# A hybrid layer pair on one core: the S5 stage in a written order without GpSimd, its Toeplitz matrices built through DRAM, and edits at both ends

## The chip, the cores and the metric

The kernel runs on one core of a Trainium2 chip. A core has five engines that run side by side: TensorE (PE, matrix products), VectorE (DVE), ScalarE (ACT), GpSimd (POOL) and SyncE (SP), which here only issues transfers; ACT issues a few as well. Engines wait for each other by semaphores, and each runs its own list of instructions strictly in order. The metric is the time of one execution on the device in microseconds (us).

## The reference

Depth is 2: one layer of native sparse attention (NSA), one S5 layer (a diagonal state-space mixer), and a last RMS norm, for 256 positions of width 1024, all in fp32. Cut to what the change touches:

```python
h = x + nsa(rmsnorm(x, l0_norm))                  # layer 0
xn = rmsnorm(h, l1_norm)                          # layer 1
u, z = split(xn @ w_in, 2)                        # 1024 columns each
# 64 groups of 16 columns, 64 complex states each: x_t = ab * x_{t-1} + bb @ u_t
y = real(C @ x_t) + d_skip * u
y = gelu(y)
ga, gb = split(y @ w_glu, 2)
h = h + (ga * sigmoid(gb) * silu(z)) @ w_out
out = rmsnorm(h, final_norm)
```

## The kernel before, in words

All products run on PE. A large product is done from fp32r pairs: the weights (`raw`, 512 KB pieces, four buffers) are split into a high part `wh` (an ACT copy, L207) and a low part `wl` (a subtraction, L209, on the engine whose turn it is in the list `lo_eng`), the activations likewise, and three products (L224 to L226, or L244 to L246 where the weights are the moving side) stand for one of full precision. Three buffers of `wh` and of `wl` go round. Products in plain fp32 (L267, 200 of them in the program, nearly all 128 by 256) use the raw weights as they are. Most of the program is ordered per engine by a scheduler at build time; inside a `manual_schedule` block the named engines keep the order of the code.

The attention layer fills the span to about 240 us. S5's parameters (the discretised states, the powers of the state matrix, `kt_` with the taps of each group) are worked out behind it by a background generator on POOL, DVE and small PE products; C's transposes (L544) are among them.

The S5 stage, from 242 us to the first product of `w_glu`:

- `u` in two halves of 512 columns (`proj_N`). Each half is transposed by DVE from PSUM and multiplied with the norm's row factors (L1368, L1369) into `ut`.
- A sequence is cut into chunks of 8 positions. Inside a chunk the contribution of `u` to `y` is one product with a Toeplitz matrix per group, `tm`. 32 transfers of SP (L1181) build `tm` out of `kt_`, SBUF to SBUF, in pieces of 64 to 512 bytes per row.
- From `ut` the inputs `v` of the scan come by products (L1305), an ACT copy `vs` (L1308), PE transposes (L1312) and copies on ACT and DVE (L1319, L1321). `scan_half` for each half of the groups (L1338 to L1358) rotates them, runs two first-order scans on DVE (L1344, L1345), rotates back (one multiplication on POOL, L1348) and writes the states `xf`.
- `z` in four tiles of 256 columns (`proj_T`, 48 products each), each scaled by DVE out of its PSUM bank (L1392), then tanh on ACT and a multiplication on DVE. In this stretch `lo_eng` is POOL alone.
- `y` in eight pieces (L1410 with the states, L1411 with `tm`), each transposed by DVE (L1413), gelu on ACT (L1416), split by DVE (L1417) and POOL (L1418).
- Then the products of `w_glu` (four pairs of tiles `gb`, `ga`), those of `w_out`, and the last norm with its stores.

The first norm (L332 on) squares both halves of x on ACT, and runs two chains of one-column DVE operations for the inverse root. The last norm multiplies with the norm's weights (`hg`, POOL) before the row factor is known, and stores the second half of the rows in eight pieces (L1469, L1471).

## Time and profile before

| | |
|---|---|
| median of 3 runs | 413.06 us (411.81, 413.06, 414.19) |
| the profiled execution | 414.05 us, its span 412.3 us |
| mean granted TensorE clock | 0.933 of full speed |
| busy, share of the span | PE 86%, DVE 55%, ACT 43%, POOL 65% |
| PE, from 258 to 334 us | waits of 19.7 us in all |
| PE, from 345 to 387 us | busy throughout |

Times on the trace count from the start of the span. What lies outside the span in the profiled execution is 414.05 - 412.3 = 1.75 us. A bracket at the end of a trace row gives the engine's idle time before it and what ended that. The clock is given as a share of 2.4 GHz: 0.50 is the lower of its two levels, 1.2 GHz.

### The profile page before, as it was taken

To read this page: it belongs to the slowest core of one execution; us is meant where nothing else is said; L and a number is where in the kernel's file an instruction comes from. 1 tells how busy PE (TensorE), PEld (TensorE's weight loads), DVE (VectorE), ACT (ScalarE), POOL (GpSimd) and SP (SyncE) were. 2 spreads that over 40 slices of the span, in tenths; PEclk is the share of its full clock that TensorE was granted. 3 is DMA by queue.
4 is the path that set the end of the run, shared out by engine and by line. 5 is a ranking of instruction groups with operands and counts; after the bars stand their busy time and mean duration, and the time that the engine had idled before them with its cause. 6 is when DMAs were issued, how large, how long until landed. Compare 5 with 4: busy or idle time off the path is not lost.

```text
span 412.3 us, 6834 instructions
## 1 busy us (share of the span) xinstructions
PE 354.2 (86%) x2505; PEld 293.0 (71%) x2505; DVE 227.9 (55%) x582; ACT 178.4 (43%) x397; POOL 269.3 (65%) x281
## 2 busy tenths in 40 slices
PE   3899599999999998968998879994858599999990
PEld 3688468865888787644766657783847599999890
DVE  4969904433355243524555498563999944264243
ACT  3212420145366467566784454342513335444432
POOL 7009459989987789999544489321872476665760
PEclk9699979999999999985999999998696899999996
DMA  8964315558633315411311335996741215655403
GB/s 256 158 172 114 110 53 153 152 190 244 181 103 99 106 57 178 126 52 51 103 36 58 113 103 99 172 87 180 251 156 54 71 34 158 199 163 200 152 2 102
DMA packets 59970, 52.03 MB, mean 126 GB/s; under 512 B 21928, under 2 KB 52704, under 8 KB 59872
## 3 DMA queue, kind: packets, MB, share of 16 engines
q1 hardware_dynamic: 49536, 50.41, 43.9%
q10 hardware_dynamic: 10400, 1.18, 2.2%
q8 instruction: 20, 0.33, 0.4%
q14 instruction: 14, 0.11, 0.1%
HBM read 48.17 MB, written 1.05 MB: 119 GB/s over the span
## 4 chain that ended last, share of the span: by engine, by line
PE 57%; DVE 16%; SPq 6%; POOL 6%; DMA 5%; issue 5%; ACT 3%; DVEq 0%; ACTq 0%; POOLq 0%
PE b L267 16%; SPq L1181 5%; PE b L280 4%; PE b L224 4%; PE b L225 4%; PE b L226 4%; PE ob L986 3%; PE tu L973 2%; PE b L246 2%; PE b L244 2%; PE b L245 2%; DVE pw L377 2%; POOL wl L209 2%; PE cm L745 2%; DVE bbT L1357 2%
## 5 line engine op out<-in xcount | busy, mean ns | idle before, releaser
L209 POOL TENSOR_TENSOR wl<-raw,wh 128x1024 fp32r<-128x1024 f32 x30 | 74.3, 2480 | 48.3 <-ACT wh L207 48.1
L267 PE MATMUL b<-xn,raw 128*128 128x256 f32 (+1 forms) x400 | 94.9, 390 | 4.7 <-DVE kl L795 3.4
L267 PEld LDWEIGHTS b<-xn,raw 128*128 128x128 f32 (+1 forms) x400 | 74.1, 190 | 18.6 <-issue 4.6
L207 ACT ACTIVATE wh<-raw 128x1024 fp32r<-128x1024 f32 x48 | 50.8, 1058 | 67.0 <-PE b L225 20.7
L209 DVE TENSOR_TENSOR wl<-raw,wh 128x1024 fp32r<-128x1024 f32 x18 | 26.3, 1462 | 26.3 <-ACT wh L207 26.3
L959 ACT ACTIVATE pt<-pt,nm 128x128 f32<-128x128 f32 (+1 forms) x64 | 28.3, 444 | 24.8 <-DVE nm L955 24.7
L225 PE MATMUL b<-yl,wh 128*128 128x256 f32 x128 | 36.1, 283 | 0.0
L224 PE MATMUL b<-yh,wh 128*128 128x256 f32 x128 | 36.1, 284 | 0.0
L226 PE MATMUL b<-yh,wl 128*128 128x256 f32 x128 | 36.0, 283 | 0.0
L975 DVE COPY pT<-tu 128x512 f32<-128x512 f32 x24 | 16.6, 691 | 25.4 <-PE tu L973 24.7
L968 ACT ACTIVATE pt<-pt,su 128x128 f32<-128x128 f32 (+1 forms) x64 | 24.6, 443 | 11.6 <-DVE su L966 11.5
L224 PE MATMUL b<-xp,wh 128*128 128x256 f32 x64 | 20.2, 317 | 5.7 <-ACT wh L207 5.7
L224 PEld LDWEIGHTS b<-yh,wh 128*128 128x128 f32 x128 | 24.5, 192 | 0.2 <-issue 0.2
L225 PEld LDWEIGHTS b<-yl,wh 128*128 128x128 f32 x128 | 24.6, 192 | 0.0
L226 PEld LDWEIGHTS b<-yh,wl 128*128 128x128 f32 x128 | 24.5, 192 | 0.0
L383 POOL TENSOR_TENSOR ep<-c1c,pw 128x1024 f32<-128x1024 f32 x8 | 16.0, 2022 | 10.3 <-ACT c1c L546 5.3
L955 DVE CUSTOM_DVE_ANT_0 pt<-su,b 128x128 f32<-128x128 f32 (+1 forms) x64 | 19.4, 351 | 4.7 <-PE su L943 4.7
L226 PE MATMUL b<-xp,wl 128*128 128x256 f32 x64 | 20.1, 316 | 1.6 <-POOL wl L209 1.6
L383 POOL TENSOR_TENSOR bbn<-bbn,bbt 128x512 f32<-128x512 f32 x16 | 20.4, 1274 | 0.6
L383 POOL TENSOR_TENSOR bbn<-b1c,h 128x512 f32<-128x512 f32 x16 | 17.8, 1111 | 4.6 <-PE bg L604 4.4
L986 PE MATMUL ob<-pT,vsw 128*64 128x128 f32 x192 | 17.4, 297 | 3.4 <-DVE pT L975 3.4
L225 PE MATMUL b<-xp,wh 128*128 128x256 f32 x64 | 19.8, 311 | 0.0
(319 smaller groups left out, 874.1 us busy)
## 6 DMA issues: line engine op xcount, KB each, us to landing
raw<-in_l_w_in_dram SPq DMA_DIRECT2D x44, 512.0 KB, 4.0
raw<-in_l_w_out_dram SPq DMA_DIRECT2D x16, 512.0 KB, 3.9
raw<-in_l_w_glu_dram SPq DMA_DIRECT2D x16, 512.0 KB, 3.6
raw<-in_l_cmp_k_w_dram SPq DMA_DIRECT2D x4, 512.0 KB, 3.9
raw<-in_l_cmp_v_w_dram SPq DMA_DIRECT2D x4, 512.0 KB, 3.9
xin<-in_x_dram SPq DMA_DIRECT2D x2, 512.0 KB
h<-in_x_dram SPq DMA_DIRECT2D x8, 128.0 KB, 3.3
tm<-kt__2197 SPq DMA_DIRECT2D x4, 128.0 KB
```

The lines of the kernel that those rows point to most:

```text
L207: A.activation(hi, raw, AF.Copy)
L209: lo_eng[-1].tensor_tensor(lo, raw, hi.bitcast(F32), op=ALU.subtract)
L224: T.matmul(dst, a, xh[:, k], start=(k == 0 and e == 0), stop=False)
L225: T.matmul(dst, a, xl[:, k], start=False, stop=False)
L226: T.matmul(dst, b, xh[:, k], start=False, stop=(k == KT - 1 and e == len(dsts) - 1))
L267: T.matmul(dst, w[:, i, e * m:(e + 1) * m], xn[:, k], start=(k == 0 and e == 0), stop=(k == KT - 1 and e == len(dsts) - 1))
L383: PL.tensor_tensor(o, a, b_, op=op)
L955: V.tensor_tensor_reduce(o.rearrange("p t k -> p (t k)"), sb[:, i * w + br * nk:i * w + (br + 1) * nk], self.b8[hf][:, S - nk:S], -0.125, ...
L959: A.activation(o, o, AF.Exp, scale=-1.0, bias=self.nm[:, j, hf, br:br + 1], accum_out=self.su[:, j, hf, br:br + 1])
L968: A.activation(o, o, AF.Copy, scale=r)
L986: T.matmul(self.ob[64 * hf:64 * hf + 64, j * P:(j + 1) * P], vsw[:, kt, br, 64 * g:64 * g + 64], p_, start=first, stop=last, tile_position ...
L1181: nc.sync.dma_start(tm[16 * s_:16 * s_ + 16, 16 * j:16 * j + 16].rearrange("p q l c -> p q (l c)")[:, :, 16 * l_:P], kt_[32 * j:32 * j + 1 ...
```

## The change

First norm: the square of the second half moves to DVE, the two chains take strict turns, and the first operations of S5's parameter chain, which the scheduler had mixed in, stand behind the norm. C's transposes get PSUM banks of their own. `kt_` is laid out anew; four transfers write it to DRAM (`kd`), and eight larger ones read `tm` from there.

The S5 stage is one block in a written order on PE, ACT, DVE and POOL. Products of `u`'s second half and of `v`, the scan and `z` are interleaved by hand. Tile 0 of `z` remains an fp32r product. For tiles 1 to 3 `x1_again` transposes the residual stream once more into `xf1`, and `z_products` multiplies it with the raw weights in plain fp32, 16 products for a tile, with no splits. The scan's multiplication on POOL goes to DVE, `y` is done in four pieces of 512 columns, gelu is evaluated twice by ACT (once into the high part), the low part is DVE's, and tanh with its multiplication (`z_gate`) moves into the loop of `w_glu`. The row of the last norm's weights, `gf`, is loaded into part of `tm` there. In the tail the second half of the rows is stored by four transfers, three of them on ACT's queue.

```diff
+        sums, ys = smp.tile([P, NQ], F32, name="ss0"), [[], []]
+        A.activation(sqs[:, 0], xin[:, 0], AF.Square, accum_out=sums[:, 0:1])
+        V.tensor_tensor_reduce(sqs[:, 1], xin[:, 1], xin[:, 1], 1.0, 0.0, ALU.mult, ALU.add, sums[:, 1:2])
+        for j in range(NQ):
+            for k in range(KT):
+                T.transpose(bts[k // 2][:, k % 2, j * P:(j + 1) * P], xin[:, j, k * P:(k + 1) * P], ident)
+        rq = [rsqrt_steps(sums[:, j:j + 1], ys[j]) for j in range(NQ)]
+        T.transpose(gb0[:, :KT], nrow, ident[:KT, :KT])
+        for r in rq * 12:
+            next(r, None)
+        for j in range(NQ):
+            row_bcast(*ys[j], rb[:, j * P:(j + 1) * P], cbias[:, j, 0:8].rearrange("p h n -> p (h n)"))
+        V.tensor_copy(g0c, gb0[:, :KT])
+        V.tensor_copy(rrow, rb[:, :S])
+        for k in range(KT):
+            V.scalar_tensor_tensor(xn[:, k], bts[k // 2][:, k % 2], g0c[:, k:k + 1], rrow,
+                                   op0=ALU.mult, op1=ALU.mult)
+        s5_loads()
+        chain = chain_gen()
+        for _ in range(3):
+            next(chain)
...
-            bt2 = bg_bank()
+            bt2 = bank(("tu", "ob")[q], 1)
...
-        kt_ = xp_.tile([P, 16, P], F32, name="kt_")
+        kt_ = xp_.tile([P, L, 16, 16], F32, name="kt_")
...
-            A.activation(kt_[:, ks_], kb, AF.Copy)
-            V.tensor_tensor(kt_[:, ks_, 0:16], kt_[:, ks_, 0:16], dk[:, ks_], op=ALU.add)
+            A.activation(kt_[:, :, ks_].rearrange("p d i c -> p i d c"), kb.rearrange("p i (d c) -> p i d c", d=L), AF.Copy)
+            V.tensor_tensor(kt_[:, 0, ks_], kt_[:, 0, ks_], dk[:, ks_], op=ALU.add)
...
-    tm = sl.tile([P, GS, L, 16], F32, name="tm")
+    tm = sl.tile([P, 4, L, 16, 16], F32, name="tm")
...
+    kd = kdp.tile([4, 16, L * 256], F32, name="kd")
+
     def toep_gen():
         kt_ = sh_ld["kt"]
+        for j in range(4):
+            nc.sync.dma_start(kd[j], kt_[32 * j:32 * j + 16].rearrange("p l i c -> p (l i c)"))
+        yield
         for s_, l_ in enumerate(SLOT_L):
-            for j in range(4):
-                nc.sync.dma_start(
-                    tm[16 * s_:16 * s_ + 16, 16 * j:16 * j + 16].rearrange("p q l c -> p q (l c)")[:, :, 16 * l_:P],
-                    kt_[32 * j:32 * j + 16, :, 0:P - 16 * l_])
-                if j % 2:
-                    yield
+            nc.sync.dma_start(tm[16 * s_:16 * s_ + 16, :, l_:L].rearrange("p j l i c -> p j (l i c)"),
+                              kd[:, :, 0:(L - l_) * 256].rearrange("j p x -> p j x"))
+            if s_ % 2:
+                yield
...
+    def u_evac(cc):
+        uh = ut[:, 32 * cc:32 * cc + 32]
+        V.transpose(uh, ubs[cc].rearrange("p j (g c) -> p g j c", c=16))
+        V.tensor_tensor(uh, uh, rcolT.unsqueeze(1).to_broadcast([P, 32, NCH]), op=ALU.mult)
...
-        for q in range(2):
-            for u in range(2):
-                for ri in range(2):
+                T.transpose(vb[:, q, t * P:(t + 1) * P], vss[hg][q][:, t], ident)
+        for ri in range(2):
+            for q in range(2):
+                for u in range(2):
                     o = vh[hg][64 * u:64 * u + 64, ri, 256 * q:256 * q + 256].rearrange("p (t x) -> p t x", t=2)
                     i_ = vb[64 * ri:64 * ri + 64, q].rearrange("p (t u x) -> p u t x", u=2, x=P)[:, u]
-                    if q == 0:
+                    if q == 0 or hg:
...
-        PL.tensor_tensor(b_, c_, b_, op=ALU.mult)
         V.tensor_tensor(w2_, s_, a, op=ALU.mult)
+        V.tensor_tensor(b_, c_, b_, op=ALU.mult)
...
+    def x1_again(cc):
+        b = bank2(psu["pool"]).rearrange("p e (k s) -> p (e k) s", k=2)
+        for j in range(NQ):
+            for i in range(4):
+                T.transpose(b[:, i, j * P:(j + 1) * P], h1s[j][:, 512 * cc + i * P:512 * cc + (i + 1) * P], ident)
+        for i in range(4):
+            A.activation(xf1[:, 4 * cc + i], b[:, i], AF.Copy, scale=colsT[:, 4 * cc + i:4 * cc + i + 1])
+
+    def z_products(c2):
+        zb = bank().rearrange("p (e s) -> p e s", e=2)
+        for k0 in range(0, KT, 4):
+            w = load_w(w_in1, k0, 4, D + 256 * c2, 2 * P)
+            for i in range(4):
+                k = k0 + i
+                for e in range(2):
+                    T.matmul(zb[:, e], w[:, i, e * P:(e + 1) * P], xf1[:, k], start=(k == 0 and e == 0),
+                             stop=(k == KT - 1 and e == 1))
+        return zb
+
+    def z_scaled(c2, zb):
+        V.tensor_tensor(z2[:, 2 * c2:2 * c2 + 2], zb, rrow.unsqueeze(1).to_broadcast([P, 2, S]), op=ALU.mult)
+
+    def z_gate(c2):
+
+        th = wk.tile([P, 2, S], F32, tag="sg", name="th", bufs=2)
+        zt = z2[:, 2 * c2:2 * c2 + 2]
+        A.activation(th, zt, AF.Tanh, scale=0.5)
+        V.scalar_tensor_tensor(zt, th, 1.0, zt, op0=ALU.add, op1=ALU.mult)
...
+        V.transpose(ytf, yb)
+        A.activation(yhl[0][:, qs_], yt, AF.Gelu_apprx_tanh)
+        A.activation(yt, yt, AF.Gelu_apprx_tanh)
+        V.tensor_tensor(yhl[1][:, qs_], yt, yhl[0][:, qs_].bitcast(F32), op=ALU.subtract)
...
+    with tc.manual_schedule(engines={E_.PE, E_.Activation, E_.DVE, E_.Pool}):
+        u_evac(0)
+        for _ in range(2):
+            next(gen_u1)
+        v_products(0)
+        next(gen_u1)
+        v_transposed(0)
+        for _ in gen_u1:
+            pass
+        zb = bank().rearrange("p (e s) -> p e s", e=2)
+        gen_z = proj_T_steps([zb[:, 0], zb[:, 1]], w_in1, D, P, xh1, xl1)
+        for _ in range(4):
+            next(gen_z)
+        scans = [scan_steps(0), scan_steps(1)]
+        u_evac(1)
+        next(scans[0])
+        v_products(1)
+
+        sh_ld["xm"].__exit__(None, None, None)
+        sh_ld["bp"].__exit__(None, None, None)
+        rs.__exit__(None, None, None)
+        wk = ctx.enter_context(tc.tile_pool(name="wk", bufs=1, reuse_waits="tile"))
+        xf1 = wk.tile([P, KT, S], F32, name="xf1")
+        z2 = wk.tile([P, KT, S], F32, name="z2b")
+        x1_again(0)
+        for _ in gen_z:
+            pass
+        for _ in toep:
+            pass
+        hooks.clear()
+        x1_again(1)
+        v_transposed(1)
+        next(scans[0])
+        next(scans[0])
+        z_scaled(0, zb)
+        zb = z_products(1)
+        next(scans[1])
+        z_scaled(1, zb)
+        yb = [y_products(q2) for q2 in range(2)]
+        for q2 in range(2):
+            y_gelu(q2, yb[q2])
+        zb = z_products(2)
+        next(scans[1])
+        next(scans[1])
+        z_scaled(2, zb)
+        zb = z_products(3)
+        yb = [y_products(q2) for q2 in range(2, 4)]
+        for q2 in range(2, 4):
+            y_gelu(q2, yb[q2 - 2])
+        z_scaled(3, zb)
+    yh, yl = yhl
...
-    with tc.manual_schedule(engines={E_.PE, E_.Activation}):
-        v_half(0)
-        v_half(1)
-    for hg in range(2):
-        scan_half(hg)
-    lo_eng[:] = [PL]
...
-        zb = bank().rearrange("p (e s) -> p e s", e=2)
-        proj_T([zb[:, 0], zb[:, 1]], w_in1, D + 256 * c2, P, xh1, xl1)
-        if c2 == 0:
-            hooks.clear()
-            for _ in toep:
-                pass
-            dump("tm", tm)
-            sh_ld["xm"].__exit__(None, None, None)
-            sh_ld["bp"].__exit__(None, None, None)
-            rs.__exit__(None, None, None)
-            wk = ctx.enter_context(tc.tile_pool(name="wk", bufs=1, reuse_waits="tile"))
-            z2 = wk.tile([P, KT, S], F32, name="z2b")
-        zs = wk.tile([P, 2, S], F32, tag="zs", name="zs", bufs=1)
-        V.tensor_tensor(zs, zb, rrow.unsqueeze(1).to_broadcast([P, 2, S]), op=ALU.mult)
-        zt = z2[:, 2 * c2:2 * c2 + 2]
-        A.activation(zt, zs, AF.Tanh, scale=0.5)
-        V.scalar_tensor_tensor(zt, zt, 1.0, zs, op0=ALU.add, op1=ALU.mult)
...
-        V.transpose(yt, yb[:, :S])
...
-        V.tensor_copy(yh[:, qd], yt)
-        PL.tensor_tensor(yl[:, qd], yt, yh[:, qd].bitcast(F32), op=ALU.subtract)
...
+    lo_eng[:] = [V, V] + [PL, PL, V] * 10
...
+    gf = tmf[:, 4 * D:5 * D]
     for c2 in range(4):
+        z_gate(c2)
+        if c2 == 1:
+            nc.sync.dma_start(gf, fnorm.unsqueeze(0).to_broadcast([P, D]))
...
-        if i == 4:
+        if i >= 3:
...
-        V.scalar_tensor_tensor(ho[1][:, 768:D], h1s[1][:, 768:D], y, gf[:, 768:D], op0=ALU.mult, op1=ALU.mult)
-        V.tensor_scalar(ho[1][:, 512:768], hg[1][:, 512:768], y, None, op0=ALU.mult)
+        V.scalar_tensor_tensor(ho[1][:, 512:D], h1s[1][:, 512:D], y, gf[:, 512:D], op0=ALU.mult, op1=ALU.mult)
         for l_ in range(4):
-            nc.sync.dma_start(o3[1, l_, :, 0:512], ho[1][32 * l_:32 * l_ + 32, 0:512])
-        for l_ in range(4):
-            (nc.scalar, nc.sync)[l_ % 2].dma_start(o3[1, l_, :, 512:D], ho[1][32 * l_:32 * l_ + 32, 512:D])
+            (nc.sync if l_ == 1 else nc.scalar).dma_start(o3[1, l_], ho[1][32 * l_:32 * l_ + 32])
```

Three places show what the order becomes. The first is DVE where the first half of `u` leaves PSUM (bank `b_2189` before, `b_2191` after; the second half is `b_2453`); `wl` are the low parts, the first two of each list those for the second half's first weights. Before:

```order
L639 TENSOR_TENSOR kt__2197<-kt__2197,dk 128x4x16
L209 TENSOR_TENSOR wl<-raw,wh 128x1024 x2
L1368 STREAM_TRANSPOSE ut<-b_2189 128x1024
L209 TENSOR_TENSOR wl<-raw,wh 128x1024
L1369 TENSOR_TENSOR ut<-ut,rcolT 128x1024
L209 TENSOR_TENSOR wl<-raw,wh 128x1024
L1368 STREAM_TRANSPOSE ut<-b_2453 128x1024
```

And after:

```order
L645 TENSOR_TENSOR kt__2199<-kt__2199,dk 128x64
L1304 STREAM_TRANSPOSE ut<-b_2191 128x1024
L1305 TENSOR_TENSOR ut<-ut,rcolT 128x1024
L214 TENSOR_TENSOR wl<-raw,wh 128x1024 x3
L1334 COPY bbT_88<-b_2558 64x256 x4
L214 TENSOR_TENSOR wl<-raw,wh 128x1024 x2
L1304 STREAM_TRANSPOSE ut<-b_2453 128x1024
```

Two low parts that stood ahead of the evacuation of `u` now stand behind it, and the fourth stands behind the four copies of `v`.

The second place is ACT from the weights of `u`'s second half to those of `z`. `vs` and `bbT_88` are the two evacuations of `v`, `xf` the second transposition of the residual. Before:

```order
L1289 ACTIVATE rrow<-b_2416 128x256
L207 ACTIVATE wh<-raw 128x1024 x3
L1308 ACTIVATE vs<-b_2539 128x512
L1308 ACTIVATE vs<-b_2558 128x512
L1319 ACTIVATE bbT_88<-b_2538 64x256 x4
L1308 ACTIVATE vs<-b_2594 128x512
L1308 ACTIVATE vs<-b_2613 128x512
L207 ACTIVATE wh<-raw 128x1024
```

And after:

```order
L1296 ACTIVATE rrow<-b_2418 128x256
L1318 ACTIVATE vs<-b_2500 128x512
L1318 ACTIVATE vs<-b_2519 128x512
L212 ACTIVATE wh<-raw 128x1024
L1332 ACTIVATE bbT_88<-b_2558 64x256 x4
L212 ACTIVATE wh<-raw 128x1024 x2
L1318 ACTIVATE vs<-b_2637 128x512
L1318 ACTIVATE vs<-b_2656 128x512
L1384 ACTIVATE xf_2681<-b_2683,colsT 128x256 x4
L212 ACTIVATE wh<-raw 128x1024
```

High parts that were made in one run ahead of `v` now each stand behind an evacuation.

The third place is PE behind the first half of `z`'s tile 0 (`b_2595`), up to the first plain product of tile 1 and `y`. Before, PE went from `v` to `z` (`b_2683`) like this:

```order
L246 MATMUL b_2453<-wh,xp_2274 128x512
L1305 MATMUL b_2539<-bbT_208,ut 32x128 x12
L1305 MATMUL b_2558<-bbT_88,ut 32x128 x16
L1312 MATMUL b_2538<-ident,vs 128x128 x8
L1305 MATMUL b_2594<-bbT_88,ut 32x128 x8
L1305 MATMUL b_2594<-bbT_1040,ut 32x128 x8
L1305 MATMUL b_2613<-bbT_1040,ut 32x128 x16
L224 MATMUL b_2683<-xp_2162,wh 128x256
```

After, two pieces of its list, the first at the middle of tile 0, the second at its end:

```order
L231 MATMUL b_2595<-xp_2164,wl 128x256
L1315 MATMUL b_2637<-bbT_88,ut 32x128 x8
L1315 MATMUL b_2637<-bbT_1039,ut 32x128 x8
L1315 MATMUL b_2656<-bbT_1039,ut 32x128 x16
L1382 MATMUL b_2683<-ident,h_93 128x128 x8
L229 MATMUL b_2595<-xp_2276,wh 128x256
```

```order
L231 MATMUL b_2595<-xp_2276,wl 128x256
L1382 MATMUL b_2726<-ident,h_93 128x128 x8
L1325 MATMUL b_2739<-ident,vs 128x128 x8
L1393 MATMUL b_2767<-xf_2681,raw 128x256 x16
L1419 MATMUL b_2796<-ep,bbT_88 32x8x16
```

The products of `v`'s second half moved between the halves of tile 0, 16 transposes of the residual (L1382) are new, and a tile of `z` is one run of 16 products.

## Rows read from the trace of the kernel before

**Rows 1.** PE's waits, 258 to 334 us: total us, times, longest

```profile
PE b L1410 <- DVE zs L1392: 11.8, 2, 7.2
PE b L224 <- ACT wh L207: 5.7, 1, 5.7
PE b L226 <- POOL wl L209: 1.6, 1, 1.6
```

**Rows 2.** Windows: stretch, length, busy of each engine, clock, DMA share, GB/s

```profile
285.00:295.00 10.00, 5.79 (x25) 5.50 (x26) 5.94 (x6) 5.69 (x9) 7.32 (x4) 0.51 0.93 312
310.00:316.00 6.00, 4.69 (x33) 4.28 (x34) 6.00 (x7) 1.58 (x2) 2.95 (x1) 0.51 0.02 4
326.00:330.00 4.00, 3.49 (x75) 3.38 (x79) 3.44 (x7) 2.64 (x4) 0.68 (x1) 0.57 0.42 123
345.00:387.00 42.00, 42.00 (x325) 40.81 (x324) 14.73 (x13) 19.43 (x22) 29.20 (x14) 1.00 0.60 188
```

**Rows 3.** PE's own timeline: start, duration, instruction, idle time before

```profile
86.34 3.62 PE L267 MATMUL b<-xn,raw 128*128 128x256 f32 x16
...
271.26 1.44 PE L1312 MATMUL b<-ident,vs 128*128 128x128 f32 x8
...
281.48 0.28 PE L225 MATMUL b<-xp,wh 128*128 128x256 f32 x1
281.60 0.28 PE L226 MATMUL b<-xp,wl 128*128 128x256 f32 x1
...
333.86 0.38 PE L224 MATMUL b<-yh,wh 128*128 128x256 f32 x1
```

**Rows 4.** The page's costliest groups, the plain fp32 products

```profile
L267 PE MATMUL b<-xn,raw 128*128 128x256 f32 (+1 forms) x400 | 94.9, 390 | 4.7 <-DVE kl L795 3.4
```

**Rows 5.** SP's queue, 250 to 292 us, and the DMA packets, 248 to 300

```profile
252.86 6.59 SPq L1181 DMA_DIRECT2D tm<-kt__2197  x8
...
262.45 19.85 SPq L1181 DMA_DIRECT2D tm<-kt__2197  x22
282.40 2.19 SPq L193 DMA_DIRECT2D raw<-in_l_w_in_dram  x4
...
DMA packets 12915, 8.18 MB, mean 157 GB/s; under 512 B 7856, under 2 KB 12464, under 8 KB 12848
```

**Rows 6.** DVE's timeline, 258 to 317 us

```profile
258.23 1.24 DVE L1368 STREAM_TRANSPOSE ut<-b 128x1024 f32<-128x1024 f32 x1
259.40 1.18 DVE L209 TENSOR_TENSOR wl<-raw,wh 128x1024 fp32r<-128x1024 f32 x1
260.50 1.21 DVE L1369 TENSOR_TENSOR ut<-ut,rcolT 128x1024 f32<-128x1024 f32 x1
...
274.32 1.74 DVE L1321 COPY bbT<-b 64x256 f32<-64x256 f32 x4 [1.35 <-ACT bbT L1319]
279.12 0.69 DVE L1343 TENSOR_TENSOR bbT<-bbT 128x512 f32<-128x512 f32 x1
...
313.57 2.87 DVE L1343 TENSOR_TENSOR bbT<-bbT 128x512 f32<-128x512 f32 x1
```

**Rows 7.** POOL's timeline at the same time

```profile
312.94 2.95 POOL L209 TENSOR_TENSOR wl<-raw,wh 128x1024 fp32r<-128x1024 f32 x1 [6.76 <-ACT wh L207]
```

**Rows 8.** ACT's timeline, 268 to 275 us

```profile
268.39 1.06 ACT L207 ACTIVATE wh<-raw 128x1024 fp32r<-128x1024 f32 x1 [2.50 <-DMA raw<-in_l_w_in_dram]
...
271.40 0.60 ACT L1308 ACTIVATE vs<-b 128x512 f32<-128x512 f32 x1 [0.28 <-PE b L1305]
272.74 1.55 ACT L1319 ACTIVATE bbT<-b 64x256 f32<-64x256 f32 x4 [0.75 <-PE b L1312]
```

**Rows 9.** SP's queue, 400 us to the end

```profile
405.29 1.76 SPq L1463 DMA_DIRECT2D out_dram<-tm  x4
...
409.15 0.84 SPq L1471 DMA_DIRECT2D out_dram<-tm  x2
```

**Rows 10.** What PE waited for, whole span

```profile
PE bg L544 <- DVE pT L494: 1.2, 1, 1.2
```

More of the change, by code (lines that the diff above doesn't have):

```diff
@@ L179, in s5_loads @@
             nc.scalar.dma_start(cnat[:, :, i], cc.rearrange("(t g) c p -> (g c) t p", t=8))
+    att = tc.tile_pool(name="att", bufs=1, reuse_waits="tile")
+    atp = att.__enter__()
+    cbias = atp.tile([P, NQ, 16, NB], F32, name="cbias")
     hooks = []
```

134 lines of the change are left out of this document (54 added, 80 removed).

## The prediction

> **What bounds the kernel now.** I read the windows first. From 345 to 387 us, in the products of `w_glu` and `w_out`, PE is busy for 42.00 of 42 us [rows 2]. So whatever the stage ahead gains or loses arrives at the end nearly undiminished: the end is the first product of `w_glu`, at 333.86 us [rows 3], plus a fixed run of work. Hence the second view, what PE waited for on its way there: 11.8 us in two waits for DVE to scale `z` out of its bank, 5.7 us for a high part of weights, 1.6 us for a low part by POOL [rows 1], 19.1 us together. Third, the windows behind these waits: the clock stands at 0.51 from 285 to 295 us and from 310 to 316 us and at 0.57 from 326 to 330 us [rows 2], so that products cost twice their time there. Half of PE's busy time in them is such excess: 2.9 + 2.3 + 1.7 = 6.9 us.
>
> The views of the other engines say why PE waited. SP issued 22 of the Toeplitz transfers from 262.45 on, for 19.85 us, and the weights that `z` waited for only at 282.40; 7856 of 12915 packets were under 512 B, at a mean of 157 GB/s [rows 5]. And DVE's one addition of 128 by 512 took 0.69 us at 279.12, but 2.87 us at 313.57 [rows 6], beside POOL's split of 2.95 us [rows 7]. The scan was slow where POOL split weights, and `z`'s scaling stood behind the scan.
>
> **The change, part by part: the stage.** Counted on PE from 258 us to the first product of `w_glu`, as differences; the products of `u`, `v`, tile 0 and `y` remain.
>
> Plain `z` products. Before, a tile is 48 products that follow each other by 0.12 us (281.48 to 281.60 [rows 3]), 5.8 us. The page lists 400 rows for L267 [rows 4] where the program has 200 products: each fp32 product is two rows. So the 16 rows of 3.62 us [rows 3] are 8 products, at 0.43 to 0.45 us each, and a tile of 16 is 6.9 to 7.2 us. That is 1.1 to 1.4 us more on PE, three times: +3.4 us at the lower end. The edit saves splits, not PE.
>
> Second transposition of the residual: 16 transposes; eight took 1.44 us, the last one's tail included [rows 3]. +2.2 us.
>
> Waits. POOL's splits and the late weights go: DVE's scan runs at 0.69 us an operation, and 32 issues of SP become 12. The bytes are not fewer: eight reads of 2.4 MB at 157 GB/s [rows 5] take 15 us, at the 312 GB/s of the window at 285 [rows 2] 8 us, behind four writes. They start about 253 us, like the transfers of before [rows 5], and end by 268 to 275 us, while `tm` is wanted by `y`, about 300 us; the weights of tile 0 queue behind them and are wanted about 280 us (258 plus the products and waits below). I cost the trip through DRAM at nothing, hidden by the products of `u` and `v`; without that cover it is up to 10 us.
>
> In their place come waits that the written order makes, since a low part stands behind an evacuation on DVE, and a high part on ACT, each ahead of the next piece of PE's work. First, the second half of `u`: its first low part stands behind transpose 1.24, multiplication 1.21, then takes 1.18 [rows 6]; less 0.3 us of PE work beside, 3.2 us. Before, PE did not wait there, the low parts being ready. Second, its third weights: a copy 0.60, the high part 1.06 [rows 8], the low part 1.18, and a handing over, 3.0 us. Third, its fourth weights: four copies of 1.55 on ACT [rows 8] and four of 1.74 on DVE [rows 6] take turns, then 1.06 and 1.18, of which 0.8 overlaps; with handings over 5.0 us. Fourth, the second half of tile 0: two `vs` copies and four copies of `xf` by ACT, 2.9 us of which PE's transposes cover 1, then 1.06 and 1.18, 3.8 us. Together 15.0 us for 19.1, -4.1 us; by the rows I allow 11 to 19 us. Behind that, I see PE busy without a wait through tiles 1 to 3 and `y`: from the fourth wait to the second half's states DVE has some 34 operations of 0.7 to 1.2 us, 26 us (my estimate from [rows 6]), and PE three tiles, 20.7 us, and beside them half of tile 0 (2.9), 16 transposes (2.2) and half of `y`.
>
> Clock. The 6.9 us of excess go if no wait lets the clock fall: -6.9 us. But four waits of 3 to 5 us are the kind that made it fall before: the wait of 5.7 us and those of 7.2 and 4.6 us [rows 1] each have a half-rate window behind them [rows 2]. No row has one of 3 to 4 us here. Each fall costs 1.7 to 2.9 us, by those windows. I take 3.0 us, for one or two falls of four (0 to 9).
>
> The Trainium skill (TensorE: Matmul & The Clock Gate, HAM oscillation) says that waits between short bursts of products can throttle the engine again at every turn. By that rule all four waits cost, 9 us in place of 3, and the sum below would be 6 us higher; the trace agrees where it shows waits of 4.6 us and more.
>
> The `gf` load. ACT's scaling of that row (1.06 us by ACT's split of the same size [rows 8]) stands ahead of high parts of the second tile of `w_glu`, and its load can be issued only when PE has read `tm` for the last time. ACT, the high part behind it and POOL's low part follow one another, 1.06 + 1.06 + 2.95 [rows 7], and PE has 72 products of 0.12, 8.6 us, until it wants them. With a landing of 3.5 us that fits; with one of 8 it costs 4.5. I take 0.9, a fifth of that (0 to 5).
>
> Sum of the stage: 3.4 + 2.2 - 4.1 - 6.9 + 3.0 + 0.9 = -1.5 us.
>
> **The tail.** Before, SP issued the first rows' four stores until 407.05 and the last of the others until 409.99 [rows 9], and the span ended 2.3 us later. Now ACT's queue issues three and SP one, when the wide multiplication is done about 406.2. At 0.44 us an issue (1.76 for four [rows 9]) both end about 407.6. -2.3 us, with the same landing; larger stores landing later could take 0.5 back.
>
> **The start.** C's transposes waited 1.2 us for a shared bank [rows 10]; with banks of their own PE goes on. The norm's chain is free of the parameter operations, which come later instead and can hold back POOL's work. I take -1.2 us, the wait alone, between -3 and +1.5, as the scheduler mixes the rest anew.
>
> Together -1.5 - 2.3 - 1.2 = -5.0 us: 409.05 us against the profiled 414.05. That execution lies 1 us above the median, so 408.0 us.
>
> **The rivals.** *The clock holds.* Waits of 3 to 5 us pass without a fall and `gf` lands early: 3.9 us less, and if three of the waits are a microsecond shorter, 6.9 less: 401 to 404 us. For it speaks that PE runs dense between the waits; against it, all rows of waits above 4.5 us.
>
> *Slower.* The clock falls at each of the four waits, since each comes within 7 us of the last and PE never recovers: 12 us of half-rate excess in place of 3, and so 9 us on the forecast: 417 us, with nothing else gone wrong. It decides when the excess passes 8 us, from where on the sum is above the old time. Against it: behind the fourth wait PE has over 26 us of dense work, and in the rows the clock was back within 10 us.
>
> *The gain is eaten in the stage.* DRAM's round trip makes tile 0's weights late by 5 us, or POOL's leftover low part holds the scan: 412 to 413 us, no change. Against it stands the room of 5 to 12 us for the load.
>
> **How the numbers follow.** A measurement of this kernel tells no change from about 0.5%, 2.07 us. The forecast, a gain of 2 to 8 us (405 to 411), has 0.47; the clock holding, or a stage better than I count, 0.24; the gain eaten 0.16; slower 0.13. Of the forecast 0.02 reaches into the middle band, so faster has 0.69, same 0.18, slower 0.13. The range leaves out the best of the second case and most of the slower one: 400.5 to 414.0 us; the forecast's own is 404 to 411.
>
> **What would show it.** Right: SP's queue done with `tm` by 264 us; no DVE addition of 128 by 512 above 1 us beside POOL; rows of a `z` tile of 16 products summing to 6.9 us at full clock; PE waiting for low parts four times between 258 and 295 us, 3 to 5 us each; the last store issued about 2.3 us sooner after the last product. The clock in the windows behind each wait decides between the cases. Wrong: PE waiting for `xf` or a bank in tiles 2 and 3 (DVE is then the bound), `tm`'s landing after 290 us, or waits by PE of over 5 us in `w_glu`'s first tiles behind `gf`.

## The result, and the profile after

The changed kernel is slower: 426.2 us (median of 4, 424.55 to 429.0) against 412.83 (4 runs, 411.81 to 414.19) beside it on the same chip, a ratio of 1.0322 (95% interval 1.0294 to 1.0351). Forecast were 408.0 us, within 400.5 to 414.0. The profiled execution took 425.98 us, its span 424.2. Of the runs below, two of e1's four executions, one of e6's four (the one that was profiled, so its trace is not read) and one of e13's six lay more than 1.5% above the fastest of their kernel, and their times and ratios are given without these.

To see where the 11.9 us of span went, I read the same seven events in both traces, in us from the start of the span. The last column is by how much the stretch that ends there grew.

| event | before | after | stretch |
|---|---|---|---|
| first product of the first projection | 13.11 | 11.83 | -1.3 |
| PE goes on after its wait for `kl`, the keys' low parts | 50.58 | 58.42 | +9.1 |
| PE's wait for `nm` ends, in late attention | 187.97 | 195.73 | -0.1 |
| last broadcast behind `u`'s first half | 257.56 | 268.20 | +2.9 |
| first product of `w_glu` | 333.86 | 340.87 | -3.6 |
| last residual addition starts | 402.73 | 413.76 | +4.0 |
| end of the span | 412.3 | 424.2 | +0.9 |

So the S5 stage, to which most of the prediction went, did become shorter. The loss lies in the start (+7.8 net of the faster norm), in late attention, in `w_glu` and at the end.

**The start.** DVE's timeline ahead of `kl`, before:

```profile
47.13 0.43 DVE L377 TENSOR_TENSOR c<-pw 128x256 f32<-128x256 f32 x1
47.59 0.42 DVE L377 TENSOR_TENSOR pw<-pw,c 128x256 f32<-128x256 f32 x1
48.05 0.63 DVE L532 COPY h<-pw 128x128 f32<-128x128 f32 x4
```

The same operations after:

```profile
49.07 0.41 DVE L339 TENSOR_TENSOR pw<-pw,c 128x256 f32<-128x256 f32 x1
...
49.85 2.13 DVE L339 TENSOR_TENSOR c<-pw 128x256 f32<-128x256 f32 x1
52.02 2.13 DVE L339 TENSOR_TENSOR pw<-pw,c 128x256 f32<-128x256 f32 x1
54.18 2.34 DVE L538 COPY h<-pw 128x128 f32<-128x128 f32 x4
```

GpSimd's timeline there, before and after, a row each (three such products follow one another, in 5.97 and 6.37 us):

```profile
48.62 2.02 POOL L383 TENSOR_TENSOR ep<-c1c,pw 128x1024 f32<-128x1024 f32 x1 [5.33 <-ACT c1c L546]
```
```profile
49.66 2.04 POOL L345 TENSOR_TENSOR ep<-c1c,pw 128x1024 f32<-128x1024 f32 x1 [3.65 <-DVE pw L339]
```

And what PE waited for, before and after:

```profile
50.58 4.90 PE L267 MATMUL b<-xn,raw 128*48 128x256 f32 x11 [3.43 <-DVE kl L795]
```
```profile
58.42 1.91 PE L272 MATMUL b<-xn,raw 128*48 128x256 f32 x4 [12.42 <-DVE kl L798]
```

Before, GpSimd starts 0.02 us after DVE's `kl`, which begins at 48.60, when the last table operations are done. After, it starts at 49.66, ahead of them, and they last as long as its own products, 2.13 us in place of 0.42. `kl` stands behind them on DVE, and PE waits 12.42 us.

So it is not that GpSimd starts earlier: it starts 1.0 us later than before. Before, what released it last was ACT's `c1c`, which ended at 48.49 us; in the changed kernel `c1c` ends at 48.60, but the table comes 2.7 us later (its last `c<-pw` begins at 47.13 and at 49.85), and now GpSimd is ahead of the table's end. The two rows of 2.13 and the one of 2.34 us are 5.1 us longer than before; with the 2.7 that is the whole 7.8.

The trace of before shows the same meeting further up in the same chain. Two equal operations of the table, the second beside a product of GpSimd:

```profile
38.78 0.21 DVE L377 TENSOR_TENSOR pw<-pw,c 128x64 f32<-128x64 f32 x1
...
41.11 2.26 DVE L377 TENSOR_TENSOR pw<-pw,c 128x64 f32<-128x64 f32 x1
```
```profile
40.88 2.42 POOL L383 TENSOR_TENSOR h<-h,ep 128x1024 f32<-128x1024 f32 x1
```

**The stage.** PE's waits from 268.2 to 340.87 us (engine, line, what for: us in all, times, longest), where before had those of [rows 1]:

```profile
PE b L249 <- ACT wh L212: 5.3, 2, 3.6
PE b L250 <- DVE wl L214: 4.8, 3, 3.3
PE b L229 <- ACT wh L212: 2.6, 1, 2.6
PE b L231 <- DVE wl L214: 0.8, 1, 0.8
```

Four waits, 13.5 us together; the single ones of 0.8 come right behind one for a high part. Tile 1 of `z`, and tiles 2 and 3, on PE's timeline:

```profile
312.45 7.07 PE L1393 MATMUL b<-xf,raw 128*128 128x256 f32 x32
323.16 14.08 PE L1393 MATMUL b<-xf,raw 128*128 128x256 f32 x64
```

SP's transfers of the Toeplitz matrices, of which 22 were issued until 282 us in [rows 5]:

```profile
261.87 2.36 SPq L1186 DMA_DIRECT2D kd<-kt__2199  x4
267.74 3.60 SPq L1189 DMA_DIRECT2D tm<-kd  x8
```

**`w_glu`.** ACT's scaling of `gf`, and the two waits of PE behind it:

```profile
348.10 1.06 ACT L1518 ACTIVATE tm<-tm 128x1024 f32<-128x1024 f32 x1 [4.14 <-DMA tm<-in_final_norm_dram]
```
```profile
350.16 0.39 PE L229 MATMUL b<-yh,wh 128*128 128x256 f32 x1 [0.39 <-ACT wh L212]
352.60 0.39 PE L231 MATMUL b<-yh,wl 128*128 128x256 f32 x1 [1.93 <-POOL wl L214]
```

These waits are 2.3 us, and behind them the clock falls (start and end, length, busy time of PE and the other engines, PE's granted clock, DMA share, GB/s). Half of PE's busy time there, 1.7 us, is lost too; the two make the 4.0 us of this stretch:

```profile
354.01:357.43 3.42, 3.42 (x19) 3.42 (x18) 3.42 (x3) 1.04 (x1) 1.86 (x1) 0.50 0.91 278
```

**The end.** The last additions on DVE, and the issues of the stores on SP and on ACT's queue (before: [rows 9]):

```profile
412.57 1.02 DVE L1527 TENSOR_TENSOR h<-b,h 128x512 f32<-128x512 f32 x2 [6.89 <-PE b L1564]
413.76 0.42 DVE L1527 TENSOR_TENSOR h<-b,h 128x256 f32<-128x256 f32 x1 [0.17 <-PE b L1564]
```
```profile
417.20 2.07 SPq L1539 DMA_DIRECT2D out_dram<-tm  x4
419.38 1.08 SPq L1544 DMA_DIRECT2D out_dram<-tm  x1
```
```profile
417.82 1.47 ACTq L1544 DMA_DIRECT2D out_dram<-tm  x3
```

The additions that the code spreads over the last products come all at once, so the first rows' four stores are issued in the same moment as the second rows'.

### The profile page after: what moved, and what is told of

Same layout as the page of the kernel before. It is cut to its first block, busy times and chain, and to the rows that moved or that the text cites. A ratio compares the mean times of both kernels' runs of the same rounds, so it can differ in the third digit from the quotient of the medians.

```text
span 424.2 us, 6710 instructions
## 1 busy us (share of the span) xinstructions
PE 360.1 (85%) x2473; PEld 295.9 (70%) x2473; DVE 217.3 (51%) x576; ACT 176.4 (42%) x401; POOL 235.7 (56%) x261
## 4 chain that ended last, share of the span: by engine, by line
PE 66%; DVE 10%; POOL 6%; issue 6%; ACT 5%; DMA 4%; SPq 0%; ACTq 0%; DVEq 0%; POOLq 0%
PE b L272 17%; PE b L1393 5%; PE b L231 4%; PE b L229 4%; PE b L230 4%; PE b L250 4%; PE b L249 3%; PE b L251 3%; PE ob L989 3%; PE tu L976 3%; DVE pw L339 2%; POOL wl L214 2%; POOL bbn L345 2%; DMA ep<-in_l_c_re_dram 2%; PE b L285 2%
## 5 line engine op out<-in xcount | busy, mean ns | idle before, releaser
L214 POOL TENSOR_TENSOR wl<-raw,wh 128x1024 fp32r<-128x1024 f32 x21 | 50.6, 2409 | 60.5 <-ACT wh L212 60.5
L212 ACT ACTIVATE wh<-raw 128x1024 fp32r<-128x1024 f32 x42 | 44.2, 1056 | 50.5 <-PE b L230 14.4
L214 DVE TENSOR_TENSOR wl<-raw,wh 128x1024 fp32r<-128x1024 f32 x21 | 29.0, 1391 | 36.6 <-ACT wh L212 36.6
L1393 PE MATMUL b<-xf,raw 128*128 128x256 f32 x96 | 21.2, 380 | 0.0
L1393 PEld LDWEIGHTS b<-xf,raw 128*128 128x128 f32 x96 | 18.1, 190 | 2.5 <-issue 0.2
L249 PE MATMUL b<-wh,xp 128*128 128x512 f32 x32 | 14.7, 461 | 5.3 <-ACT wh L212 5.3
```

What stands on the lines that cost most here:

```text
L212: A.activation(hi, raw, AF.Copy)
L214: lo_eng[-1].tensor_tensor(lo, raw, hi.bitcast(F32), op=ALU.subtract)
L249: T.matmul(dst, a, wh[:, i], start=(k == 0 and not (one_bank and j > 0)), stop=False)
L1393: T.matmul(zb[:, e], w[:, i, e * P:(e + 1) * P], xf1[:, k], start=(k == 0 and e == 0), stop=(k == KT - 1 and e == 1))
```

## The experiments

### The start: which of its two edits

My theory at that point: banks of their own let C's transposes, and so GpSimd's products, come earlier, while the norm's edit makes the table later; they meet. The rival: the norm's edit alone. Five kernels take the two edits apart.

**e1: the changed kernel, C's transposes back on the shared bank.**

```diff
-            bt2 = bank(("tu", "ob")[q], 1)
+            bt2 = bg_bank()
```

> The changed kernel with one edit undone: C's transposes share the background generator's PSUM bank again. Theory A (GpSimd's three multiplications with C's transposes now start at 49.7 us, beside the last additions of DVE's power table, and slow these from 0.4 to 2.1 us each): the shared bank makes GpSimd start about 51.3 us, DVE's operations of 128 by 256 take 0.4 us again, the keys' low parts start about 51.4 instead of 56.4, PE resumes about 53.3 instead of 58.4, and the time falls by 5 us to about 421. Rival B (the keys are late only because the parameter chain now stands behind the first norm): PE resumes about 58 us as in the changed kernel, and the time stays at 426.

Measured 417.45 and 420.49 us (2 runs), ratio 1.0136 (1.008 to 1.0191). GpSimd's and PE's rows:

```profile
50.19 6.02 POOL L345 TENSOR_TENSOR ep<-c1c,pw 128x1024 f32<-128x1024 f32 x3 [5.22 <-ACT c1c L552]
```
```profile
52.26 3.92 PE L272 MATMUL b<-xn,raw 128*48 128x256 f32 x11 [2.99 <-DVE kl L798]
```

DVE's table operations take 0.43 us again. They stand 1.0 us earlier than in the changed kernel and GpSimd starts 0.5 us later, now behind them; and PE goes on 6.2 us earlier.

**e2: the changed kernel with the first norm of before** (own banks stay). **e3:** this and the shared bank. The edit, cut:

```diff
-        V.tensor_tensor_reduce(sqs[:, 1], xin[:, 1], xin[:, 1], 1.0, 0.0, ALU.mult, ALU.add, sums[:, 1:2])
+            A.activation(sqs[:, j], xin[:, j], AF.Square, accum_out=sums[j])
...
-        for r in rq * 12:
+        for _ in range(6):
+            next(rq[0])
+        for r in (rq[1], rq[0]) * 12:
...
-        for _ in range(3):
-            next(chain)
```

> The changed kernel with the first norm of before (both squares on ACT, parameter operations mixed in); C's banks stay its own. Theory A: DVE's chain is 2.7 us earlier, but GpSimd starts with it and still slows its last operations: PE resumes about 55.7, the time is 423 to 424. Rival B: PE resumes about 50.6 as in the kernel before, the time is 418.

> The changed kernel with both edits of the start undone. Both theories: PE resumes about 50.6 us, the time falls by 7.8 us to about 418.4; if the other 2.8 us that are lost by the end of the first half of u also come from the start, 415.6. What is left above the kernel before (412.8) then belongs to w_glu and the tail, less what the S5 stage gains.

e2 measured 414.62 us (10 runs), 1.0024 (1.0 to 1.0048); e3 415.25 (10 runs), 1.0049 (1.0018 to 1.0079). PE goes on at 49.64 and 49.87 us. So with the old norm the banks do no harm: in e2 GpSimd starts at 47.69 and DVE's last table operations ran before. Late attention takes 69.1 and 69.2 us in the two, so its 2.9 us come from the norm's edit as well. My expectation for e2, 55.7 us, was wrong.

**e4: the kernel before with own banks alone. e6: the kernel before with the first norm of the changed one alone.** (e4's edit is that of e1 the other way round, e6's that of e2.)

> The kernel before with one edit alone: own banks for C's transposes. Theory A: GpSimd starts about 47 us, DVE's last operations slow to 2 us, PE resumes about 55.7 instead of 50.6, and the kernel is slower by about 5 us, 418. Rival B: no change, 412.8, or faster by the 1.2 us that these transposes waited.

> The kernel before with the edit of the first norm alone (square on DVE, chains in turn, the parameter chain behind it). If the parameter chain's displacement is the loss and GpSimd's start keeps its shield (C's transposes share the bank), PE resumes at about 52.3 us as in the run with the shared bank, the late attention takes the same 2.5 us more, and the kernel is slower by 4 to 7 us, 418 to 420. If the edit only costs together with the banks, there is no change, 413.7.

e4: 413.74 us (10 runs), 0.9992 (0.997 to 1.0013), no change; GpSimd starts at 51.20, behind the table. The table ends late in this trace, and GpSimd starts late with it: in all eight traces with the norm of before, `kl` begins somewhere between 47.7 and 51.2 us, and GpSimd 0.02 to 0.04 us behind it. e6: 419.95 us (3 runs), 1.0151 (1.0106 to 1.0196). The norm's edit alone costs 6.8 us (419.95 against 413.17), as expected, and the banks alone cost nothing. In which way the norm's edit costs this with a shared bank, the time alone does not say.

### The row `gf` and the stores

**e5: the changed kernel, `gf` in a buffer that is free earlier.**

```diff
-    gf = tmf[:, 4 * D:5 * D]
+    gf = xf1.rearrange("p k s -> p (k s)")[:, 0:D]
+    nc.sync.dma_start(gf, fnorm.unsqueeze(0).to_broadcast([P, D]))
...
-        if c2 == 1:
-            nc.sync.dma_start(gf, fnorm.unsqueeze(0).to_broadcast([P, D]))
```

> The changed kernel, with the row of the last norm loaded into the tile xf1, which is free once z's last tile is done, so about 3.5 us earlier and ahead of the third pair of w_glu's weights in SP's queue. If ACT's wait for that load is what w_glu lost, PE's waits of 0.4 and 1.9 us at its start and the clock's fall behind them go, from w_glu's first product to the last addition it takes 68.9 us again instead of 72.9, and the time falls by 4 us to 422. If the turn of GpSimd and DVE in splitting w_glu's weights is the cause, the 72.9 us stay.

Measured 422.18 us (4 runs), 1.0227 (1.0185 to 1.0269): 4.0 us less than the changed kernel. Both waits are gone (one of 0.8 us for a low part of `y` is left); from the first product of `w_glu` to the last addition it takes 69.7 us (before 68.9, after 72.9), 3.2 us less.

The load in its old place does not always cost as much. In the changed kernel, e1 and e2, ACT began to scale the row 6.6 to 6.9 us after the load's issue; PE waits 2.3 to 2.5 us, the clock falls, and the stretch takes 72.9 to 73.1 us. In e3, e9 and e13, which have the same load, ACT began 5.3 to 5.8 us after it; PE waits 1.1 to 1.5 us, the clock holds, and the stretch takes 69.9 to 70.3 us, hardly more than with the repair.

**e7: the kernel before with the new stores alone.**

```diff
-            nc.sync.dma_start(o3[1, l_, :, 0:512], ho[1][32 * l_:32 * l_ + 32, 0:512])
-        for l_ in range(4):
-            (nc.scalar, nc.sync)[l_ % 2].dma_start(o3[1, l_, :, 512:D], ho[1][32 * l_:32 * l_ + 32, 512:D])
+            (nc.sync if l_ == 1 else nc.scalar).dma_start(o3[1, l_], ho[1][32 * l_:32 * l_ + 32])
```

> The kernel before with the edit of the tail alone. My forecast's term: the last store is issued 2.3 us sooner and the time falls by 2.3 us to 411.4. The rival, from the changed kernel's trace (10.4 us from the last addition to the end instead of 9.6): larger stores land later, and the time is the same or up to 0.9 us longer.

Measured 412.11 us (10 runs), 0.9971 (0.9949 to 0.9993): -1.06 us (413.17 beside it), where I had counted -2.3. The issues on ACT's queue and on SP end earlier:

```profile
404.52 1.32 ACTq L1468 DMA_DIRECT2D out_dram<-tm  x3
```
```profile
403.46 1.75 SPq L1463 DMA_DIRECT2D out_dram<-tm  x4
405.33 0.36 SPq L1468 DMA_DIRECT2D out_dram<-tm  x1
```

The last ACT issue ends at 405.84, 4.95 us after the last addition (400.89), where before it was SP's, 7.26 us after: the 2.3 us that I had counted. But the span ends 3.9 us behind it, at 409.7, against 2.3 before. The stores, now 1024 columns wide, land later by most of what their earlier issue gained. Whether that is their size, or that all eight stores of the end are now issued within 2.4 us on two queues, this run does not separate.

**e8: the changed kernel with the norm of e2 and the row of e5.**

> The changed kernel with the first norm of before and the last norm's row loaded into xf1: both losses taken out. The run with the norm of before stood at 414.6; without the wait in w_glu 4 us less, about 410.5, which is what the S5 stage, the trip through DRAM and C's banks are worth together with the new tail. If the losses overlap, 412 to 414.

Measured 412.31 us (10 runs), 0.9994 (0.9975 to 1.0013): the two repairs bring the kernel back to the time of before, and no further. From the last addition to the end it takes 10.56 us, where e7 has 8.81.

### What was still missing

**e9: the changed kernel with the parameter operations left to the scheduler. e10: e8 with PE in the order of the code through the last products. e11: both, and `gf` as in e5. e12: the kernel before with the S5 stage alone.**

```diff
-        chain = chain_gen()
-        for _ in range(3):
-            next(chain)
```
```diff
-    for ch in range(4):
-        ws.append(stream(w_out1, 2 * ch, 2, 512, 512))
+    with tc.manual_schedule(engines={E_.PE}):
+        for ch in range(4):
+            ws.append(stream(w_out1, 2 * ch, 2, 512, 512))
```

> The changed kernel with its first norm (square of the second half on DVE, strict turns), but with the first operations of S5's parameter chain left to the scheduler again, in place of standing in a block behind the norm. Theory A, that this place of the parameter operations makes the power table late and brings DVE's last table operations beside GpSimd's products: PE resumes after its wait for the keys' low parts at about 50 us, not 58.4, DVE's operations there take 0.43 us again, and the time is 413 to 416 us. Theory B, that the turns or the square on DVE delay the chain: PE resumes at 56 us or later and the time stays at 423 to 426 us.

> The changed kernel with the first norm of before and the row of the last norm's weights loaded elsewhere (412.3 us measured), and now with PE kept in the order of the code through the last products of w_out, where the scheduler had mixed the products of the last two column pieces. Theory A, that this mixing costs the tail its gain: from the last residual addition to the end 8.8 us in place of 10.6, with that addition no later than by 0.2 us, so 410.5 to 411 us. Theory B, that the late end comes from the larger stores alone: 412.3 us, no change.

> The changed kernel with three repairs: the parameter operations free, the row of the last norm's weights loaded elsewhere, PE in the order of the code through the last products. If theory A of the run with the chain free and theory A of the run with the last products in order both hold: 409 to 411 us, about 1 us below the latter, as the norm with strict turns reaches the first projection 1.3 to 2 us sooner. If the norm's turns are what is slow: 417 to 420 us.

> The kernel before with the S5 stage of the changed kernel alone (the row of the last norm's weights loaded elsewhere; first norm, shared bank for C's transposes and last stores as before). Theory A, by the traces of the runs so far, in which the stage from the last broadcast of u's first half to the first product of w_glu is 0.8 to 1 us shorter than before and the rest alike: 412.0 to 412.8 us. Theory B, by the prediction's sum for the stage without the row's load, -2.4 us: 410.5 to 411 us.

e9: 419.66 us (6 runs), 1.016 (1.0122 to 1.0198), between the two theories. PE goes on at 53.92; the table's `pw` and `c` are free, but its last copies still meet GpSimd:

```profile
47.72 4.30 DVE L535 COPY h<-pw 128x128 f32<-128x128 f32 x4
```
```profile
47.86 6.06 POOL L345 TENSOR_TENSOR ep<-c1c,pw 128x1024 f32<-128x1024 f32 x3 [4.91 <-ACT c1c L549]
```

e10: 411.5 us (12 runs), 0.9945 (0.9923 to 0.9967), the lowest median of all versions. Its stores are issued as in e7, and the stretch from the last addition to the end is 8.82 us, as expected; its time is 0.5 us above the expected range. So the scheduler's mixing of the last two column pieces, not the stores themselves, is what made that stretch longer than e7's.

e11: 418.1 us (6 runs), 1.0111 (1.008 to 1.0142), 6.6 us above e10, from which it differs by the norm alone: so more than the place of the parameter operations is at fault in that edit. e12: 413.13 us (12 runs), 0.9999 (0.9974 to 1.0024): the stage alone brings nothing that can be measured. Its trace says where the gain goes: the stage is 1.2 us shorter (75.1 for 76.3), but `w_glu` takes 70.2 us for 68.9, with a wait of 1.3 us for a low part of `y`, and the end 11.3 for 9.6, since here too the last additions come together, with the stores of before. So this edit also reorders the last products, and e12 charges the stage with it.

**e13: the changed kernel, GpSimd held behind the table. e14: e11 with the second half's square on ACT. e15: e14 with GpSimd held as well.**

```diff
+        PL.tensor_copy(ep[:, 0, 0, :].rearrange("p (r l) -> p r l", r=2), pws[:, :, :, 0])
+
         GE = 8
```
```diff
-        V.tensor_tensor_reduce(sqs[:, 1], xin[:, 1], xin[:, 1], 1.0, 0.0, ALU.mult, ALU.add, sums[:, 1:2])
+        A.activation(sqs[:, 1], xin[:, 1], AF.Square, accum_out=sums[:, 1:2])
```

> The changed kernel with one addition: ahead of its long products on c1c, GpSimd copies 16 elements out of the last table that DVE writes, so that it cannot start beside DVE's last table operations. Theory A, that these run 2.1 us instead of 0.42 because GpSimd's products run beside them: they take 0.42 to 0.6 us again, GpSimd starts at 51 to 52 us in place of 49.7, PE resumes at about 53 us in place of 58.4, and the time is 420.5 to 421.5 us (426.2 without the copy). Late attention stays at 72.5 us, since PE's order there is unchanged. Theory B, that DVE is slow there for another reason, or that GpSimd's later start is lost again further on: PE resumes at 57 us or later, or the time stays above 424 us.

> The changed kernel with the three repairs (418.1 us measured), and the square of the second half of x on ACT again; the strict turns stay. In the order of the instructions PE's list from the first scores of attention on is then that of the run with the first norm of before, row by row, where the three repairs have another. Theory A, that the square's place makes the scheduler arrange late attention worse: the stretch from the wait for nm to the last broadcast of u's first half takes 69 to 69.6 us in place of 73.4, and the time is 413.5 to 414.5 us if PE still resumes at 54 to 56 us, 410 to 411 if the square also brought on the late table. Theory B, that the stretch is long for another reason (the clock, or GpSimd's work arriving late): 72 us or more there, and 417 to 418.5 us.

> The run before this one with GpSimd's copy of 16 elements ahead of its products as well. If the collision on the table is all that makes the start late: PE resumes at 50 to 52 us, DVE's table operations take 0.42 us, and the time is 410 to 411.5 us, not below the 411.5 us of the kernel with the first norm of before by more than a microsecond, as the norm's 1.3 us are hidden behind the table. If the table is late by itself: 412 to 414 us.

e13: 418.08 us (5 runs), 1.0148 (1.0111 to 1.0185), 2.4 us below the expected range. DVE's rows, and PE's:

```profile
49.36 0.43 DVE L339 TENSOR_TENSOR c<-pw 128x256 f32<-128x256 f32 x1
49.82 0.43 DVE L339 TENSOR_TENSOR pw<-pw,c 128x256 f32<-128x256 f32 x1
50.28 0.63 DVE L538 COPY h<-pw 128x128 f32<-128x128 f32 x4
```
```profile
52.81 5.03 PE L272 MATMUL b<-xn,raw 128*48 128x256 f32 x16 [7.29 <-DVE kl L800]
```

Only GpSimd's copy was added, and the operations that took 2.13 us take 0.43: the collision is shown. PE goes on 5.6 us earlier (52.81 for 58.42): 5.1 us are the collision, and 0.5 a table that came that much sooner in this trace. That is within what traces differ: e5, with the start of the changed kernel and the same collision, has PE go on at 56.85. What the time gained beyond the expected lies in `w_glu`, where this trace has one wait of 1.1 us in place of 2.3, and 69.9 us to the last addition in place of 72.9, though its load of `gf` was not touched.

e14: 411.67 us (12 runs), 0.997 (0.9953 to 0.9988); e15: 411.86 (12 runs), 0.9972 (0.9948 to 0.9995). Moving one square back took 6.4 us from e11. PE goes on at 50.76 us, where e11 has 55.76, and late attention takes 69.7 us, where e11 has 73.4. So of what e11 has of the norm's edit, it is the square on DVE that costs, at both places; the strict turns stay in e14. PE's waits there, in the changed kernel and in e14:

```profile
PE bg L640 <- ACT kt__2199 L644: 3.6, 2, 2.9
PE su L945 <- DVE nm L958: 2.0, 2, 1.6
PE ob L989 <- DVE pT L978: 1.9, 3, 0.8
PE tu L976 <- ACT pt L971: 1.2, 1, 1.2
...
PE tu L976 <- DVE pT L978: 0.9, 1, 0.9
```
```profile
PE ob L986 <- DVE pT L975: 3.4, 5, 0.8
PE bg L637 <- ACT kt__2199 L641: 3.2, 2, 2.5
PE su L942 <- DVE nm L955: 1.6, 1, 1.6
```

In all 10.8 us against 9.2. The windows of 8 us that begin 55 us behind `nm`, in the changed kernel and in e14, add the clock:

```profile
250.73:258.73 8.00, 7.43 (x84) 5.82 (x84) 7.14 (x23) 2.89 (x5) 7.61 (x15) 0.79 0.20 68
```
```profile
243.13:251.13 8.00, 7.28 (x91) 5.83 (x90) 7.93 (x20) 3.40 (x7) 7.69 (x13) 1.00 0.21 72
```

0.21 of 7.43 us is 1.6 us; with the waits' difference, 1.6, that is 3.2, for 2.8 us measured. PE's instructions show what the square, some 180 us earlier, had done there: the scheduler lists the transposes of `pt` in another order (a piece of the difference, e11 with -, e14 with +; ahead of late attention they differ almost only in where small transposes stand among the first projections' products):

```
 L942 MATMUL su<-kh,qs 128x256
-L943 MATMUL su<-kl,qs 128x256
-L942 MATMUL su<-kh,qs 128x256
+L973 MATMUL tu<-ident,pt 128x128
+L943 MATMUL su<-kl,qs 128x256
+L973 MATMUL tu<-ident,pt 128x128
+L942 MATMUL su<-kh,qs 128x256
+L973 MATMUL tu<-ident,pt 128x128
```

The six traces read here with the square on DVE have 71.7 to 74.6 us there, all the others 69.0 to 69.7. In the six PE is idle for 8.7 to 9.1 us of it and loses 5.1 to 8.3 us to the clock (half of its busy time at the lower one), in the others 7.8 to 7.9 and 3.6 to 4.3: the waits differ by about 1 us, the clock by 1 to 4. That the square's place does this is shown by e14; that it does so through the order of the `pt` transposes is argued from the list and not tested. Holding GpSimd in e15 changed nothing more, as e14 no longer collides.

## Why the prediction was wrong

**The reading of before was right**: PE's waits in the stage and the half-rate clock behind them, and an end that moves with the first product of `w_glu`.

**The step that failed is the start**, the term of -1.2 us, "the wait alone, between -3 and +1.5". It measured +7.8 us to `kl` (5.1 of collision, 2.7 of a later table) and +2.9 in late attention. I looked at what the edit removes (1.2 us of a bank's wait, which by e4 gains nothing alone) and wrote that displaced operations "can hold back POOL's work", but not what they run beside. The trace had the answer: GpSimd began 0.02 us after the operation behind the table, and a DVE addition took 2.87 us beside GpSimd [rows 6, 7], which I had used for the stage and not for the start; the table's own rows had it too, 0.21 us alone and 2.26 beside GpSimd. The Trainium skill (SBUF — State Buffer, two separate sides) has the rule: a DVE operation with two SBUF inputs, or in a mode that uses two ports, takes one port pair in turns with a GpSimd operation that reads SBUF, each for a whole instruction. The trace agrees: 2.13 us for the DVE operation beside GpSimd products of 2.04. Late attention I had not considered at all, although the text says that the scheduler "mixes the rest anew".

**The `gf` load**, 0.9 us (0 to 5), cost 4.0 by e5's time and 3.2 by its trace. SP issued it at 341.48 and ACT could start 6.6 us later, between the two landings that I had weighed, 3.5 and 8. 2.3 us are waits; 1.7 are the clock behind them, which the term did not have. The sign, the place and the upper bound were right. The size differs between the traces: with the same load, e3, e9 and e13 lose little more than 1 us, close to the 0.9. No row had given either landing, so the share that I took between them was a guess.

**The tail**, -2.3 us, is -1.1 alone (e7), because the new stores land 1.6 us later where I allowed 0.5; in the changed kernel it became +0.9, because the scheduler took the last products out of order (e10 shows it).

**The stage**, -2.4 us without `gf`. Most terms held one by one: a plain `z` tile 7.07 us (6.9 to 7.2), SP done with `tm` at 271.3, which without the 10.6 us of shift ahead of the stage is before the 264 forecast, and no wait for `tm`, no wait in tiles 2 and 3, four waits for high and low parts of 13.5 us in all (15.0). They took 3.3, 2.5, 4.4 and 3.4 us; the parts that I listed for the first and the fourth add up to 3.3 and 4.1, not to the 3.2 and 3.8 that I wrote. DRAM's round trip was hidden, as I had costed it. What varied is the clock. The same block, with the same four waits, takes 71.3 to 72.9 us in six profiles of its 13 and 75.1 to 75.6 in the other seven, where before had 76.3. Two traces show the difference. The stretches at the lower clock in e10 (72.5 us):

```profile
260.64:264.06 3.42, 3.04 (x7) 2.46 (x8) 1.47 (x2) 0.00 (x0) 0.00 (x0) 0.50 0.98 108
281.12:284.54 3.42, 3.23 (x8) 2.55 (x9) 1.36 (x2) 1.06 (x1) 0.00 (x0) 0.50 1.07 375
294.78:298.19 3.41, 2.96 (x14) 2.96 (x15) 3.41 (x5) 0.00 (x0) 0.00 (x0) 0.50 0.47 150
```

and in e8 (75.6 us):

```profile
259.31:266.14 6.83, 6.16 (x15) 4.81 (x16) 1.75 (x2) 0.00 (x0) 0.00 (x0) 0.50 1.03 117
272.96:276.38 3.42, 3.23 (x8) 2.55 (x9) 0.14 (x1) 0.00 (x0) 0.00 (x0) 0.50 1.10 129
283.20:286.62 3.42, 3.42 (x8) 2.74 (x9) 1.07 (x1) 0.00 (x0) 0.00 (x0) 0.50 0.63 193
296.86:300.27 3.41, 3.08 (x14) 3.08 (x15) 3.41 (x5) 0.00 (x0) 0.00 (x0) 0.50 0.47 152
```

Half of PE's busy time in them is the excess, as in the prediction: 1.5 + 1.6 + 1.5 = 4.6 us in e10, three falls; 3.1 + 1.6 + 1.7 + 1.5 = 7.9 us in e8, a fall behind every wait, the first of them twice as long. I had taken 3.0, and before had 6.9. So of the clock's forecast gain of 3.9 us 2.3 are left in the one, and the other loses 1.0. The waits gave more than forecast, 19.7 - 13.5 = 6.2 us for 4.1, and what remains, the products, cost some 4.6 for 5.6. By these numbers e10's stage is 3.8 us shorter than before and e8's 0.7; that the forecast of -2.4 lies between them is partly luck, since each of the three terms missed by 1 us or more, and not all one way. All 13 traces fall into three groups: 7.4 to 7.9 us of excess in the seven long ones, 4.6 to 5.1 in four, and 3.3 in e9 and e11, with falls behind the last two waits alone.

That is the mechanism of my second rival. The rule that the prediction cited from the Trainium skill (TensorE: Matmul & The Clock Gate, HAM oscillation) holds in e8, with 7.9 us where I had worked out 9 for four falls, but not in e10, whose second wait passes without one. This mechanism is not what made the kernel slower, since at its worst the stage still is 0.7 us shorter than before. Why one trace loses the clock behind the second wait and another does not stays open: the stage's instructions and waits are the same in e8 and e10. With one trace of each kernel, whether the kernel or the execution decides can't be told.

**The range** left out what decided. Its upper end was made of the stage's unknowns; the start was given 1.5 us upwards where a collision with DVE's last table operations cost 5.1 us and a later table 2.7.

## What to carry to other kernels

An edit that moves small operations needs a look at what other engines do beside the new place: here GpSimd began 0.02 us behind the operations that its products slow down, and once these came later than its start, that cost 5.1 us on a chain that PE waits for. In a program that a scheduler orders, read the order of every engine to the end and not only around the edit; here a square on another engine cost about 3 us some 180 us later, and the last products came out of order. Split a change into its parts before believing any: the version with the lowest median (e10, 411.5 us, 0.9945 of before) keeps the stage, C's banks and the stores, leaves the norm alone, loads `gf` early, and pins the last products. e14, 411.67 us, which also keeps the norm's strict turns, cannot be told from it; and the new stores alone (e7) were 0.9971.
